# Raising the scheduling priority of attention steps by 300 places in a two-layer hybrid mixer

## The chip, the cores and the metric

The kernel runs on one core of a Trainium2 chip. The metric is device time in microseconds (us). A core has TensorE (PE, with its weight loads as PEld), VectorE (DVE), ScalarE (ACT), GpSimd (POOL) and SyncE (SP, here the issuer of most transfers). Each engine works through its own list of instructions in the order in which the compiler's scheduler wrote it down, and waits at the head of that list for semaphores.

## The reference

Two layers of a mixer on 512 tokens of x (plus 256 tokens of context), width 1024. Each layer projects the normalised input with `w_in`, runs three mixers side by side, gates them, and multiplies with `w_out`:

```python
oa = _rms(_diff_attend(qa, ka, va, lam), da_subln_g) * (1.0 - lam_init)
ob = _rms(_gqa_attend(qg, kg, vg).reshape(B, L, GQ_WIDTH), gq_out_g)
oc = _rms(_hyena(uh, filt, hy_short_w, hy_short_b, hy_bias), hy_out_g)
y = jnp.concatenate([oa * jax.nn.silu(ga), ob * jax.nn.silu(gg), oc * jax.nn.silu(gh)], axis=-1)
return y @ w_out
```

`_diff_attend` (DA below) has 4 heads whose attention matrix is softmax minus lambda times a second softmax; `_gqa_attend` (GQA) has 8 query heads over 2 key heads; `_hyena` is a gated long convolution, done here by matrix products. In layer 0 the context is a query too, in layer 1 only x is. Keys are the context and x together, 768 of them for a query of x.

## The kernel before

The work is float32, done as three matmuls on a high and a low half of each operand (lines L138, L139, L140 of `mm3`); `split` and `evac_split` make the halves, ACT the high one and DVE or POOL the low one (L152, L156, L581, L582). A layer's function projects one weight block after another (`proj_tok` into tiles named `pst`, `proj_feat` into `psf`), and after the last block multiplies the mixed heads with `w_out` into tiles named `px`.

Attention is written as generators. `gq_att` and `da_att` do one head and one block of 256 queries per step: scores `S` (six matmuls for each half block in DA, L628 and L629; nine in GQA), a maximum on DVE (L634), the exponential into `P` on ACT (L637), then `pv`. For each of three pairs of key blocks, `pv` transposes `P` with four matmuls into `T` (L648), splits `T` on ACT into `ph` (L581) and on DVE into `pl` (L582), and adds four matmuls from `ph` (L655, L656) and two from `pl` (L658) to `O`. In DA, `O` is squared on ACT (L972), read once more by DVE (L974), and a matmul `ms` (L977) sums squares over the partitions; `ms` uses the buffer of `O`. The pools `pT` and `pO` have one buffer each (L91, L92): a second `T` waits until both splits of the first are done, a new `O` until `ms` has been read.

Who comes first is settled in two stages. The code is traced in a fixed order: `att.tock()` at the head of each projection lets one or more attention steps be traced between projections, by a pace that `att.spread` sets; `slow.tick()` inside an attention step traces a piece of the modulation for the next layer; `bg` and `pre` hold hyena and next-layer work; `att.drain()` empties what is left before the `w_out` part. The scheduler then lists the instructions of each engine: of those that it holds ready it takes the one with the highest priority, and priority is the place in the traced order, the earlier the higher. So a projection traced after an attention step still comes ahead of it where the step's inputs are not there yet.

The `w_out` part reads the heads back from DRAM: `yT` tiles for blocks 0 to 7 by POOL's transfers straight to their place (L1089, L1094), blocks 8 to 14 by SP's transfers into `yld` (L1100), split by ACT (L1082) and DVE or POOL.

```python
            for i, kp in enumerate(klist):
                T = pT.tile([128, 2, 256], F32, tag="T", name="T")
...
                evac_split(ph, pl, T)
```

Of the kernel before, what the change touches and what calls it, by code (L numbers as in the profile page):

```python
# [3 lines left out]

# [30 lines left out]
class Background:  # L35


    def __init__(self):
        self.queue = deque()
        self.pace = self.due = 1.0  # L40

    def add(self, gen):
        self.queue.append(gen)
# [11 lines left out]
    def tick(self):  # L55
        while self.queue:
            try:
                next(self.queue[0])
                return
            except StopIteration:  # L60
                self.queue.popleft()
# [7 lines left out]
def hybrid_mixer(ctx: ExitStack, tc: tile.TileContext, a, out):  # L69
# [50 lines left out]

    bg = Background()
    slow = Background()
    att = Background()
    pre = Background()

    def col(l, c, n=1):
# [1372 lines left out]
```

## Time and profile before

| what | value |
|---|---|
| median of three runs | 1597.02 us (1595.21 to 1600.0) |
| the profiled execution, its own time | 1593.43 us |
| its span | 1591.7 us |
| mean granted clock of TensorE | 0.989 |
| PE busy | 1510.1 us, 95% |

The profiled execution is 3.6 us under the median, so a sum made against it stands 3.6 us lower than the time of a run. PE is the engine that is nearly always busy: 81.6 us of the span are left in which no matmul runs, and a gain or a loss by another order of the same work is a change of these 81.6 us.

### The profile page before, as it was taken

How to read it: one execution, taken by the hardware profiler on the slowest of the kernel's cores; microseconds unless marked ns; L12 is line 12 of the kernel's file. 1: busy time of each engine (PE TensorE's matmuls, PEld its weight loads, DVE VectorE, ACT ScalarE, POOL GpSimd, SP SyncE). 2: the span in 40 equal slices, each digit the busy share in tenths (PEclk: the TensorE clock that was granted, in tenths of full speed). 3: DMA queues.
4: the chain of work that ended last, by engine and by line, in shares of the span. 5: the costliest groups of instructions: out<-in, count | busy, mean ns of one | idle time of the engine just before them, and what ended most of it. 6: DMA issues, size and time to landing. Idle time of an engine off the chain costs nothing.

```text
span 1591.7 us, 29098 instructions
## 1 busy us (share of the span) xinstructions
PE 1510.1 (95%) x11126; PEld 1398.6 (88%) x11126; DVE 1127.6 (71%) x2222; ACT 830.9 (52%) x1673; POOL 415.6 (26%) x451
## 2 busy tenths in 40 slices
PE   5989999999999999998999999999999999898997
PEld 3768889999898989798999977888999998898997
DVE  6789667877776475777755378869877756768755
ACT  5645243555556555566653256334546556656643
POOL 0243443212212141113002114334222222214032
PEclk9999999999999999999999999999999999999999
DMA  9437676423435253315352334674422232115441
GB/s 344 145 111 263 192 222 200 129 76 96 143 102 169 93 159 117 113 48 195 117 179 94 93 108 145 213 229 146 152 75 87 87 97 87 57 51 182 130 133 70
DMA packets 105952, 216.87 MB, mean 136 GB/s; under 512 B 11345, under 2 KB 54291, under 8 KB 105812
## 3 DMA queue, kind: packets, MB, share of 16 engines
q1 hardware_dynamic: 95300, 178.56, 34.9%
q0 software_dynamic: 9936, 35.39, 7.3%
q8 instruction: 88, 1.44, 0.4%
q10 hardware_dynamic: 576, 1.05, 0.2%
q14 instruction: 52, 0.43, 0.1%
HBM read 174.45 MB, written 40.52 MB: 135 GB/s over the span
## 4 chain that ended last, share of the span: by engine, by line
PE 79%; DVE 9%; DMA 4%; issue 3%; ACT 3%; POOL 1%; SPq 0%; POOLq 0%; DVEq 0%; ACTq 0%
PE psf L138 7%; PE psf L139 7%; PE psf L140 7%; PE pst L138 6%; PE pst L140 6%; PE pst L139 6%; PE px L138 4%; PE px L140 4%; PE px L139 4%; PE T L648 4%; PE O L658 2%; PE O L655 2%; PE O L656 2%; PE S L138 2%; PE S L140 2%
## 5 line engine op out<-in xcount | busy, mean ns | idle before, releaser
L138 PE MATMUL psf<-hT,wh 128*128 128x512 f32 (+1 forms) x768 | 267.9, 353 | 8.8 <-DVE cv L687 5.0
L138 PE MATMUL pst<-wh,hT 128*128 128x256 f32 x960 | 273.8, 285 | 0.2
L139 PE MATMUL pst<-wl,hT 128*128 128x256 f32 x960 | 273.7, 285 | 0.0
L140 PE MATMUL pst<-wh,hT 128*128 128x256 f32 x960 | 273.6, 285 | 0.0
L139 PE MATMUL psf<-hT,wh 128*128 128x512 f32 (+1 forms) x768 | 268.4, 350 | 0.0
L140 PE MATMUL psf<-hT,wl 128*128 128x512 f32 (+1 forms) x768 | 268.2, 349 | 0.0
L156 DVE TENSOR_TENSOR wl<-raw,wh 128x1024 fp32r<-128x1024 f32 x136 | 174.6, 1285 | 40.1 <-ACT wh L152 38.7
L152 ACT ACTIVATE wh<-raw 128x1024 fp32r<-128x1024 f32 x136 | 143.5, 1056 | 90.1 <-PE psf L139 34.7
L140 PEld LDWEIGHTS pst<-wh,hT 128*128 128x128 f32 x960 | 183.9, 192 | 1.7 <-issue 1.7
L138 PEld LDWEIGHTS pst<-wh,hT 128*128 128x128 f32 x960 | 184.0, 192 | 1.6 <-issue 1.1
L139 PEld LDWEIGHTS pst<-wl,hT 128*128 128x128 f32 x960 | 183.9, 192 | 0.2
L138 PE MATMUL px<-wh,yT 128*128 128x256 f32 x640 | 181.6, 284 | 1.1 <-DMA yT<-yx 0.6
L140 PE MATMUL px<-wh,yT 128*128 128x256 f32 x640 | 181.6, 284 | 0.2 <-DVE yT L1083 0.2
L139 PE MATMUL px<-wl,yT 128*128 128x256 f32 x640 | 181.5, 284 | 0.0
L637 ACT ACTIVATE P<-S,sa 128x768 f32<-128x768 f32 (+1 forms) x160 | 130.2, 814 | 87.3 <-DVE sa L634 59.1
L138 PEld LDWEIGHTS psf<-hT,wh 128*128 128x128 f32 x768 | 146.3, 191 | 29.0 <-ACT kH L1029 3.2
L140 PEld LDWEIGHTS psf<-hT,wl 128*128 128x128 f32 x768 | 146.5, 191 | 17.9 <-issue 0.8
L139 PEld LDWEIGHTS psf<-hT,wh 128*128 128x128 f32 x768 | 146.9, 191 | 17.3 <-issue 1.2
L634 DVE TENSOR_REDUCE sa<-S 128x1 f32<-128x768 f32 (+1 forms) x160 | 134.6, 841 | 21.8 <-PE S L140 11.9
L582 DVE TENSOR_TENSOR pl<-T,ph 128x512 fp32r<-128x512 f32 x156 | 107.1, 687 | 49.0 <-ACT ph L581 44.2
L581 ACT ACTIVATE ph<-T 128x512 fp32r<-128x512 f32 x156 | 92.7, 594 | 86.5 <-PE T L648 85.6
L138 PEld LDWEIGHTS px<-wh,yT 128*128 128x128 f32 x640 | 122.1, 191 | 2.1 <-ACT pm L1152 0.9
(300 smaller groups left out, 3559.8 us busy)
## 6 DMA issues: line engine op xcount, KB each, us to landing
raw<-in_w_in SPq DMA_DIRECT2D x104, 512.0 KB, 4.1
adaw<-in_ada_w SPq DMA_DIRECT2D x32, 512.0 KB, 4.4
raw<-in_w_out SPq DMA_DIRECT2D x32, 512.0 KB, 3.8
tab<-in_inv POOLq DMA_DIRECT2D x20, 512.0 KB, 4.6
tab<-in_fwd POOLq DMA_DIRECT2D x18, 512.0 KB, 5.1
adaw<-in_ada SPq DMA_DIRECT2D x16, 512.0 KB, 10.7
yT<-yx POOLq DMA_DIRECT2D x16, 512.0 KB, 7.1
gl<-gd SPq DMA_DIRECT2D x60, 128.0 KB, 2.3
```

The lines of the kernel that those rows point to most:

```text
L138: i0 = PE.matmul(ps, sh, mh, start=first, stop=False)
L139: PE.matmul(ps, sh, ml, start=False, stop=False)
L140: return i0, PE.matmul(ps, sl, mh, start=False, stop=last)
L152: ACT.activation(hi, src, AF.Copy)
L156: last_lo[0] = e.tensor_tensor(out=lo, in0=src, in1=hi.bitcast(F32), op=ALU.subtract)
L581: ACT.activation(dh, ps, AF.Copy)
L582: return DVE.tensor_tensor(out=dl, in0=ps, in1=dh.bitcast(F32), op=ALU.subtract)
L634: DVE.tensor_reduce(out=nm, in_=S[:, :n], axis=AX.X, op=ALU.max, negate=True)
L637: ACT.activation(P[:, :n], S[:, :n], AF.Exp, bias=nm, accum_out=s)
L648: PE.transpose(T[:, kk, q * 128:(q + 1) * 128], aa[q][:, (2 * i + kk) * 128:(2 * i + kk + 1) * 128], ident)
L655: PE.matmul(O, vh, ph[:, kk], start=(i == 0 and kk == 0), stop=False)
L656: PE.matmul(O, vl, ph[:, kk], start=False, stop=False)
```

## The change

`Background` gets a tile context and a lift. Each step that the attention queue traces runs under a priority raised by 300 places, so everything that it traces (scores, softmax, transposes, the O matmuls, its loads and stores, and what `slow.tick()` adds in it) is ranked as if it stood 300 instructions earlier in the traced order. The three other queues keep a lift of 0. No instruction is added or taken away; line numbers behind L59 grow by two.

```diff
-    def __init__(self):
+    def __init__(self, tc=None, lift=0):
         self.queue = deque()
         self.pace = self.due = 1.0
+        self.tc, self.lift = tc, lift
...
             try:
-                next(self.queue[0])
+                with self.tc.high_priority(offset=self.lift) if self.lift else nullcontext():
+                    next(self.queue[0])
                 return
...
-    att = Background()
+    att = Background(tc, 300)
```

The lists of the engines differ from layer 0's first attention step on; between the two layers' attention they are nearly alike. Two places show how.

PE near the end of layer 1, the last two query blocks of DA, before: after the last transpose into `T_18296` come 26 matmuls of the w_out part (`px`), and then the O matmuls that read its high half `ph_18301`.

```order
L648 MATMUL T_18296<-ident_243,P_18242 128x128
L139 MATMUL px_18704<-wl_18693,yT_18455 128x256
L140 MATMUL px_18704<-wh_18692,yT_18455 128x256
L138 MATMUL px_18704<-wh_18692,yT_18457 128x256
...
L139 MATMUL px_18704<-wl_18687,yT_18447 128x256
L140 MATMUL px_18704<-wh_18686,yT_18447 128x256
L655 MATMUL O_18265<-ph_18301,vh_17443 128x256
L656 MATMUL O_18265<-ph_18301,vl_17444 128x256
L655 MATMUL O_18265<-ph_18301,vh_17443 128x256
L656 MATMUL O_18265<-ph_18301,vl_17444 128x256
```

On PE at the same place of the changed kernel, `px_18704` and `px_18807` have been done already, and the transposes, the O matmuls and the next transposes follow each other:

```order
L650 MATMUL T_18296<-ident_243,P_18210 128x128
L650 MATMUL T_18296<-ident_243,P_18242 128x128
L657 MATMUL O_18265<-ph_18301,vh_17443 128x256
L658 MATMUL O_18265<-ph_18301,vl_17444 128x256
L657 MATMUL O_18265<-ph_18301,vh_17443 128x256
L658 MATMUL O_18265<-ph_18301,vl_17444 128x256
L650 MATMUL T_18389<-ident_243,P_18333 128x128
L650 MATMUL T_18389<-ident_243,P_18365 128x128
L650 MATMUL T_18389<-ident_243,P_18333 128x128
L650 MATMUL T_18389<-ident_243,P_18365 128x128
L660 MATMUL O_18265<-pl_18302,vh_17443 128x256 x2
L650 MATMUL T_18404<-ident_243,P_18333 128x128
```

What moved: the px matmuls went ahead of the attention's last blocks, and nothing is left between a transpose and the matmuls that need its two splits. In the changed order no px stands between any of `T_18296`, `T_18389`, `T_18404`, `T_18419` and the O matmuls that follow; in that of before 15 or more stand behind each of the four.

ACT in layer 0, at the turn from projections to the w_out part, before: the split of the first loaded tile, `yT_10077<-yld_10075`, stands behind the exponential of `P_9402`, in front of the split `ph_9268` of an attention's transposes.

```order
L1029 ACTIVATE kH_9382<-kH_9382 64x256
L972 ACTIVATE sq_9111<-O_9095 128x256
L637 ACTIVATE P_9402,sa_9403<-S_9393,sa_9400 128x768
L1082 ACTIVATE yT_10077<-yld_10075 128x512
L581 ACTIVATE ph_9268<-T_9263 128x512
L978 ACTIVATE sq_9111<-ms_9115,epst_246 128x256
L637 ACTIVATE P_9416,sa_9417<-S_9407,sa_9414 128x768
L979 ACTIVATE sq_9111<-sq_9111 128x256
L1082 ACTIVATE yT_10082<-yld_10080 128x512
```

On ACT at the same place of the changed kernel both splits of loaded tiles stand in front of exponentials:

```order
L967 ACTIVATE P_9221<-P_9221,sa_9226 128x768
L1084 ACTIVATE yT_10077<-yld_10075 128x512
L639 ACTIVATE P_9239,sa_9240<-S_9230,sa_9237 128x768
L980 ACTIVATE sq_9111<-ms_9115,epst_246 128x256
L981 ACTIVATE sq_9111<-sq_9111 128x256
L1084 ACTIVATE yT_10082<-yld_10080 128x512
L639 ACTIVATE P_9253,sa_9254<-S_9244,sa_9251 128x768
L967 ACTIVATE P_9253<-P_9253,sa_9258 128x768
L639 ACTIVATE P_9402,sa_9403<-S_9393,sa_9400 128x768
L1014 ACTIVATE qT_9573<-pst_9513 128x512
L639 ACTIVATE P_9416,sa_9417<-S_9407,sa_9414 128x768
L583 ACTIVATE ph_9268<-T_9263 128x512
```

What moved: `yT_10077` stands ahead of the exponentials of `P_9239`, and `yT_10082` ahead of that of `P_9253`, both of an earlier attention step than before. On SP, `yld_10075` was issued directly after the load `gl_9045`; in the changed list it stands behind a weight load and the store `yx0_9<-y_8891`, which waits for POOL.

Elsewhere on PE: after `T_14039` (GQA, layer 1) stood 25 rows of matmuls before its O matmuls, now none; after `T_14407` 19, now none; after `T_15587` 23, now none; `T_14182` follows the transposes before it with two rows between. Between the last projection matmul of `pst_9318` and its own transposes (DA, layer 0) stood 45 rows of matmuls, now 13.

## Rows read from the trace of the kernel before

**Rows 1.** the page: busy time, share and instructions of each engine.

```profile
PE 1510.1 (95%) x11126; PEld 1398.6 (88%) x11126; DVE 1127.6 (71%) x2222; ACT 830.9 (52%) x1673; POOL 415.6 (26%) x451
```

**Rows 2.** windows: busy us of PE, PEld, DVE, ACT, POOL; granted clock; DMA.

```profile
300.00:400.00 100.00, 100.00 (x775) 94.75 (x773) 74.52 (x173) 56.61 (x126) 20.61 (x20) 1.00 0.34 105
...
700.00:800.00 100.00, 91.68 (x716) 88.19 (x715) 78.63 (x162) 69.84 (x147) 21.25 (x38) 0.97 0.41 133
...
1300.00:1400.00 100.00, 93.34 (x709) 88.63 (x709) 66.89 (x128) 57.55 (x109) 27.44 (x38) 0.98 0.25 79
...
1500.00:1530.00 30.00, 30.00 (x253) 29.93 (x252) 15.20 (x26) 13.12 (x25) 0.73 (x1) 1.00 0.66 203
740.00:765.00 25.00, 20.36 (x141) 18.95 (x139) 20.35 (x43) 17.58 (x35) 9.38 (x17) 0.86 0.79 264
```

**Rows 3.** what PE waited for: us in total, times, longest.

```profile
PE O L655 <- ACT ph L581: 6.2, 6, 3.0
...
PE O L658 <- DVE pl L582: 3.3, 7, 1.2
...
PE T L648 <- DVE pl L582: 1.5, 3, 0.9
```

**Rows 4.** timeline of PE: start, us, line, tiles; idle before it and releaser.

```profile
1370.82 0.60 PE L648 MATMUL T<-ident,P 128*128 128x128 f32 x4
1372.10 0.38 PE L655 MATMUL O<-ph,vv 128*128 128x256 f32 x1 [0.69 <-ACT ph L581]
...
1373.14 0.80 PE L658 MATMUL O<-pl,vv 128*128 128x256 f32 x2 [0.20 <-DVE pl L582]
```

**Rows 5.** timeline of ACT, same stretch.

```profile
1371.45 0.60 ACT L581 ACTIVATE ph<-T 128x512 fp32r<-128x512 f32 x1 [0.90 <-PE T L648]
```

**Rows 6.** timeline of DVE, same stretch.

```profile
1372.39 0.69 DVE L582 TENSOR_TENSOR pl<-T,ph 128x512 fp32r<-128x512 f32 x1
```

**Rows 7.** timeline of PE, layer 0, third attention head of DA.

```profile
746.78 0.60 PE L977 MATMUL ms<-sq,ones 128*128 128x256 f32 x2
748.00 0.39 PE L655 MATMUL O<-ph,vh 128*128 128x256 f32 x1 [0.63 <-ACT sq L978]
...
749.26 0.60 PE L648 MATMUL T<-ident,P 128*128 128x128 f32 x4
...
753.53 0.39 PE L655 MATMUL O<-ph,vh 128*128 128x256 f32 x1 [2.96 <-ACT ph L581]
```

**Rows 8.** timeline of ACT, same stretch.

```profile
751.05 0.63 ACT L1082 ACTIVATE yT<-yld 128x512 fp32r<-128x512 f32 x1 [1.92 <-DMA yld<-yx]
...
752.89 0.59 ACT L581 ACTIVATE ph<-T 128x512 fp32r<-128x512 f32 x1
```

**Rows 9.** timeline of SP: the first two loads of yld.

```profile
726.13 0.44 SPq L1100 DMA_DIRECT2D yld<-yx  x1
...
742.05 0.75 SPq L1100 DMA_DIRECT2D yld<-yx  x1
```

**Rows 10.** timeline of POOL: first and last issue of eight loads of yT.

```profile
736.94 1.14 POOL L1089 DMA_DIRECT2D yT<-yx  x2 [2.57 <-PE pst L140]
...
742.10 1.07 POOL L1089 DMA_DIRECT2D yT<-yx  x2
```

**Rows 11.** timeline of PE, layer 0: last projection matmul and its transposes.

```profile
703.94 0.28 PE L140 MATMUL pst<-wh,hT 128*128 128x256 f32 x1
...
708.24 0.66 PE L1050 MATMUL pst<-ident,t 128*128 128x128 f32 x4 [1.49 <-POOL t L1046]
```

**Rows 12.** timeline of PE, layer 1: two waits outside the round trips.

```profile
1326.30 0.47 PE L138 MATMUL psf<-hT,wh 128*128 128x512 f32 x1 [1.04 <-DVE kL L1027]
...
1333.90 0.39 PE L138 MATMUL S<-kk,qh 128*128 128x256 f32 x1 [0.74 <-ACT P L637]
```

**Rows 13.** timeline of PE, layer 1: the turn at ms.

```profile
1435.52 0.40 PE L658 MATMUL O<-pl,vh 128*128 128x256 f32 x2
...
1438.10 0.70 PE L977 MATMUL ms<-sq,ones 128*128 128x256 f32 x2 [1.31 <-DVE y L974]
```

More of the change, by code (lines that the diff above doesn't have):

```diff
@@ L2 @@
 from collections import deque
-from contextlib import ExitStack
+from contextlib import ExitStack, nullcontext
 import numpy as np
```

## The prediction

> **What bounds the kernel now.** The page's busy times come first: PE is busy for 1510.1 of 1591.7 us, 95%, DVE 71%, ACT 52% [rows 1]. The windows come next, to see where the other 81.6 us lie. Between 300 and 400 us PE has no gap at all, and in the tail at 1500 to 1530 none either; between 700 and 800 it is busy for 91.68 us and between 1300 and 1400 for 93.34 [rows 2]. So the projections alone keep PE full, and the gaps lie where the two layers' attention runs. The waits of PE name them: `O` for `ph` 6.2 us, `O` for `pl` 3.3, the next `T` for `pl` 1.5 [rows 3]. Together 11.0 us: the round trip from PE to ACT and DVE and back that each set of transposes makes. A change of order moves only gaps, so the question is which round trips have other matmuls beside them.
>
> **What a bare round trip costs.** At 1370.82 four transposes start; ACT's split starts at 1371.45 and takes 0.60, DVE's starts at 1372.39 and takes 0.69; the first O matmul starts at 1372.10 and the one from `pl` at 1373.14 [rows 4 to 6]. So `ph` is usable 1.28 us after the first transpose, `pl` 2.32 us after it, and the buffer of `T` is free again at the same moment, 2.31 us. Of this PE's own work is 0.44 (four transposes at 0.11 apart) and 0.48 (four O matmuls at 0.12): with nothing between, PE idles 0.84 us before the first O matmul and 0.56 before the `pl` pair, 1.40 in all.
>
> **The change, term by term.** No instruction is added or removed, so busy time is left as it is, and the sum is made of gaps.
>
> Round trips. I went down PE's list of each kernel, adding 0.11, 0.12 or 0.23 us for a matmul of 128, 256 or 512 columns, and held each O matmul and each next `T` to the 1.28, 2.32 and 2.31 us. Before, 23 matmuls are held up, by 9.5 us in all; the trace has 11.0 at the same waits [rows 3], so the walk is near the chip's result, a little low. After, 34 are held up, by 19.2. Where: 5.0 us in the last two query blocks of layer 1, where the lists show no px between transposes and O, and where the window was gapless [rows 2]; 4.9 in the GQA of layer 1 (1.4 each at `T_14039` and `T_15587`, 1.3 at `T_14182`, 0.8 at `T_14407`); 3.4 instead of 1.0 at the first DA head of layer 0; 2.6 less elsewhere. That is +9.7, and scaled by 11.0/9.5 it is **+11.2**. Its lower end is +9.7; its upper end takes the widest measured excess over a bare trip, 3.0 us (below), once more: +14.
>
> The Trainium skill, Perfetto Trace Analysis, section Matmuls, says that independent groups of matmuls should rotate through PSUM banks, so that the evacuation of one overlaps the next group's matmuls. The trace agrees: with one buffer for `T` there is no second transpose to start, and what hides the evacuation is other groups alone. By that rule a list that groups attention's matmuls together loses, which is the sign of the sum above.
>
> Turns at `ms`. From `ms` at 746.78 to the next O matmul at 748.00 is 1.22 us [rows 7], of which PE works 0.24: about 1.0 of idling where nothing stands between. The list of before has two such turns with under 0.5 us of work between, that of after three: **+1.2** with the shorter cover of one more.
>
> Transposes of the DA projections. Their input goes through DVE and POOL: from the last projection matmul at 703.94 to the transposes at 708.24 are 4.3 us [rows 11]. For `pst_9318` the list of after has 1.64 us of matmuls there where before had 5.6: 4.3 less 0.12 and 1.7 leaves **+2.4** (0 if the input is ready sooner than in that row, as DVE was busy with other work in it).
>
> ACT at the loaded tiles. Before, ACT stood still for 1.92 us at L1082, waiting for the load of `yld`; behind it stood a split of `T`, which began at 752.89, so that PE got its O matmul at 753.53, 4.27 us after the transposes at 749.26 [rows 7, 8]. A bare trip is 1.28: the excess is 3.0. The load was late because SP issued `yld` at 742.05 (an earlier one at 726.13) behind eight loads of 512 KB that POOL had issued from 736.94 to 742.10 [rows 9, 10], with the DMA engines at 0.79 of their time [rows 2]. After, two such splits stand ahead of exponentials of an earlier step, and the first load too is issued behind the store that waits for POOL, so into the same burst. One held load cost 3.0; I take two at 3.0 each in place of one, **+3.0**. Ends: 0 if the second load lands while ACT is held by the first, +6 if the exponentials, which stand farther from PE's matmuls than a split does, hold the scores' two buffers as well.
>
> Gains. Two waits outside the round trips, 1.04 and 0.74, stand where the list of after has scores and projections earlier: **-1.8** [rows 12]. The wait of 1.31 at `ms` [rows 13] is behind more matmuls: **-1.3**. No other cover grows where the trace had a wait.
>
> Sum: 11.2 + 1.2 + 2.4 + 3.0 - 1.8 - 1.3 = **+14.7**. Against the profiled execution that is 1593.4 + 14.7 = 1608; against the median, 3.6 us above it, **1612**. I leave the clock out of the sum: where PE idled 18% of a stretch, at 740 to 765, its granted clock was 0.86 [rows 2], so one more such stretch of 25 us costs 25 x 0.14 = 3.5 us; that goes to the range.
>
> **The rivals.**
> Faster. The lift brings attention's splits and exponentials ahead of weight splits in ACT's and DVE's lists, so that the chip's trips come to their bare length, and each trip starts sooner. For it: DVE is busy 71% and the excess at 753.53 is queueing. If all the waits for `ph` and `pl` vanished, 11.0 us would be gained: 1586. Against it: of those 11.0 the bare trips explain 9.5, so queueing is only some 1.5 of them, and a shorter queue gives no cover. It decides if the short covers of the list (34 against 23) are filled on the chip, that is if O's waits for `ph` and `pl` in the new trace are under 8 us. The Trainium skill, Perfetto Trace Analysis, section Optimization Strategy, advises to make the dependencies behind a gap start sooner; that is this rival's mechanism, and the row at 753.53 agrees with it in one place.
>
> No change. PE's gaps move: what the tail loses, an earlier place gets back, because each lifted step gives up its place to a projection of the same length. For it: the 81.6 us of gaps have many causes, and I have priced only some. Against it: it needs 10 more of gains, and I find 3.1 in the rows. Time: 1597, within 4.8 us.
>
> Much slower. ACT's two held loads take 6 instead of 3 more, PE idles over a longer stretch, and two stretches of 25 us run at 0.86: 14.7 + 3 + 7 = +25, 1622. It decides if ACT's wait for `yld` is over 4 us in total around 750.
>
> **How the numbers follow.** A measurement here can tell about 0.3%, 4.8 us, from no change. Chances: forecast (1605 to 1618) 0.53, much slower 0.20, no change 0.14, faster 0.13. Slower by over 0.3%: 0.73; within: 0.14; faster: 0.13. The range 1592 to 1628 leaves out most of the faster case below and the far end of the much slower one above; the forecast's own range is 1605 to 1618.
>
> **What would show it.** Right: O's waits for `ph` and `pl` and T's for `pl` rise from 11.0 to about 20 in the waits of PE; gaps of about 1.4 us between transposes and O in the last 20 us of attention in layer 1, where px filled them; the px part after the last O unchanged in length; a wait of ACT for `yld` in layer 0 in front of an exponential. Wrong: waits under 8 us there; PE busy over 95% between 1500 and 1530; or a new wait of 5 us or more at a place not named, most likely scores waiting for `P` or a projection waiting for a split.

## The result and the profile after

The changed kernel takes 1625.09 us (median of four runs, 1622.44 to 1627.03), the kernel before 1597.58: a ratio of 1.0171 with a 95% interval of 1.0148 to 1.0194, or 27.5 us more. The sign was forecast, and the time lies in the range of 1592 to 1628. The size was not: 14.7 us were in the sum, and the forecast's own range ended at 1618. The profiled executions differ by 33.6 us of span (1625.3 against 1591.7), since that of after was the slowest of its four runs and that of before the fastest of its own.

The page's busy times, as in [rows 1]:

```profile
PE 1527.0 (94%) x11126; PEld 1407.6 (87%) x11126; DVE 1123.4 (69%) x2222; ACT 833.0 (51%) x1673; POOL 419.0 (26%) x451
```

PE is busy for 17 us longer with the same matmuls, and the rest of the span, in which no matmul runs, went from 81.6 to 98.3 us. Not only the gaps grew, then: matmuls themselves took longer, in part because the mean granted clock fell from 0.989 to 0.983. The windows (columns as in [rows 2]), the last two between the two layers' attention:

```profile
300.00:400.00 100.00, 99.98 (x774) 94.72 (x772) 74.46 (x171) 57.01 (x127) 21.15 (x20) 1.00 0.32 103
...
700.00:800.00 100.00, 91.99 (x724) 88.94 (x723) 72.83 (x153) 63.46 (x132) 22.11 (x38) 0.97 0.39 130
1300.00:1400.00 100.00, 94.48 (x689) 88.17 (x688) 63.68 (x110) 57.04 (x102) 26.45 (x34) 1.00 0.29 92
1530.00:1560.00 30.00, 26.60 (x199) 24.73 (x198) 13.96 (x23) 13.75 (x26) 0.74 (x1) 0.94 0.60 197
1050.00:1070.00 20.00, 15.14 (x61) 12.42 (x60) 11.35 (x17) 6.93 (x10) 5.34 (x4) 0.83 0.64 212
1090.00:1110.00 20.00, 17.04 (x122) 16.87 (x121) 15.45 (x32) 6.85 (x14) 7.16 (x7) 0.83 0.49 147
```

Between 300 and 400 nothing changed, and 700 to 800 and 1300 to 1400 are no worse than in [rows 2]; the windows of 100 us cut at other places of the work, since everything slid. The tail is what the reader should compare: 30.00 of 30 before, 26.60 of 30 here at 1530 to 1560, at a clock of 0.94. Between 1050 and 1110 the clock is 0.83 in two stretches of 20 us.

What PE waited for, where [rows 3] had 6.2, 3.3 and 1.5 for `O` and `T`:

```profile
PE S L630 <- ACT P L639: 9.7, 11, 2.5
...
PE O L657 <- ACT ph L583: 7.9, 10, 1.2
...
PE yps L140 <- ACT Z L763: 4.9, 1, 4.9
PE T L650 <- DVE pl L584: 4.8, 6, 1.3
...
PE O L660 <- DVE pl L584: 2.4, 5, 0.9
...
PE pst L1052 <- POOL t L1048: 1.9, 1, 1.9
...
PE pst L140 <- DVE vl L584: 1.9, 2, 1.6
...
PE px L140 <- ACT P L639: 1.7, 1, 1.7
```

The round trips rose from 11.0 to 7.9 + 2.4 + 4.8 = 15.1 us. The largest wait is one that [rows 3] did not show: scores waiting for their buffer, which the exponential `P` must read first, 9.7 us (in the kernel before 2.9 in DA, and 1.4 in GQA, which is gone). All PE waits but those for a DMA went together from 52.6 to 71.6 us.

To see where, I took the time from each matmul's start to the next one's, less 0.109, 0.120 or 0.227 us for up to 128, 256 or 512 columns, and summed what is left over five parts of the program. It holds gaps and slow clock alike. The first row is the sum in us, the others the difference to it:

```
                      start  layer 0   between   layer 1   tail   sum
before                 24.5     15.8      19.9      20.7    0.6   81.4
after                  +1.1    +12.6      +6.0      +7.8   +6.3  +33.9
lift_layer0            -0.8    +12.3      +6.7      +2.8   -0.3  +20.7
lift_layer1            +1.7     -1.9      +0.9      +9.3   +7.5  +17.6
lift_no_drain          +0.5    +13.1      +0.5      +7.3   -0.0  +21.3
no_drain_layer1        +4.1    +12.6      +6.4      +6.5   -0.0  +29.5
store_on_pool          +2.3    +11.8      -2.6      +7.1   +5.8  +24.4
scores_unlifted        +1.1    +18.5      +2.0     +12.7   +2.3  +36.7
pv_unlifted            -1.0    +20.6      -0.0     +28.9  +11.9  +60.5
lift_30                +1.3     -4.8      +1.8      +7.0   -0.3   +4.9
lift_100               -1.3     +9.3      +3.2      +7.7   -0.0  +18.8
lift_1000              +1.4    +20.0      -0.3     +19.6  +14.6  +55.3
ysplit_pool_after      -0.4    +12.9      +1.4      +9.4   +7.4  +30.7
ysplit_pool_before     +2.1     -2.8      +2.2      +0.4   -0.1   +1.8
```

"Layer 0" is its attention and w_out part, "between" the hyena and projection work up to layer 1's first transposes, "tail" begins with the transposes of the last two query blocks. The differences fit those of the spans (33.9 and 33.6 us for the changed kernel). The expectations below speak of 9.6 and 6.5 us between the layers and of 6.5 in the tail; by this table it is 6.0 and 6.3. These are single executions: in the first part nothing is changed, and it varies by -1 to +4.

### The profile page after: what moved, and what is told of

Its sections match the earlier page's. It is cut to its first block, busy times and chain, and to the rows that moved or that the text cites. A ratio compares the mean times of both kernels' runs of the same rounds, so it can differ in the third digit from the quotient of the medians.

```text
span 1625.3 us, 29141 instructions
## 1 busy us (share of the span) xinstructions
PE 1527.0 (94%) x11126; PEld 1407.6 (87%) x11126; DVE 1123.4 (69%) x2222; ACT 833.0 (51%) x1673; POOL 419.0 (26%) x451
## 4 chain that ended last, share of the span: by engine, by line
PE 79%; DVE 8%; DMA 4%; ACT 3%; issue 3%; POOL 1%; SPq 0%; ACTq 0%; DVEq 0%; POOLq 0%
PE psf L140 7%; PE psf L141 7%; PE psf L142 7%; PE pst L140 7%; PE pst L141 7%; PE pst L142 7%; PE px L140 5%; PE px L142 5%; PE px L141 4%; PE T L650 3%; PE O L657 2%; PE O L660 2%; PE O L658 2%; PE S L140 1%; PE S L141 1%
## 5 line engine op out<-in xcount | busy, mean ns | idle before, releaser
L636 DVE TENSOR_REDUCE sa<-S 128x1 f32<-128x768 f32 (+1 forms) x160 | 134.6, 841 | 23.5 <-PE S L142 17.3
```

Source lines behind the costliest of these rows:

```text
L636: DVE.tensor_reduce(out=nm, in_=S[:, :n], axis=AX.X, op=ALU.max, negate=True)
```

## The experiments

Their line numbers lie up to four above those of the kernel before. Where an interval is given it is the 95% interval of the ratio to the kernel before, which was timed again beside each group of runs (medians of 1594.28 to 1597.58 us).

**The lift in one layer.**

```diff
         full = l == 0
+        att.lift = 300 if l == 0 else 0
```

> The lift of 300 in layer 0 only, 0 in layer 1. Theory A (lost cover: matmuls that stood inside the round trips of transposes are gone): going down PE's list by the same spacings gives 10.7 us of held-up matmuls against 9.5 before, so +1.4, with +2.4 at the transposes of the DA projections and +3 at the loaded tiles: about +7, 1604 to 1605. Theory B (PE meets a lifted instruction in its list whose inputs or buffer are not there, scores above all, and later unlifted work is reshuffled with it): the changed kernel lost 12 us at the places of layer 0's attention and 9.6 us more between the two layers' attention, where nothing is lifted; both would stay, +20, about 1618.

> The lift of 300 in layer 1 only, so that every list up to layer 1's attention is that of the kernel before. Theory A: 19.4 us of held-up matmuls against 9.5, +11.5, with +1.2 at the turn of ms: about +13, 1610. Theory B: the changed kernel lost some 11 us from layer 1's first attention step to the end, and nothing of the 9.6 us between the layers should be lost here: about +10, 1608. If the 9.6 us between the layers were not caused by layer 0's lift they would be seen here too, about 1618.

Layer 0 alone: 1616.49 us, 1.0138 (1.0118 to 1.0158). Layer 1 alone: 1609.74, 1.0087 (1.0070 to 1.0104). The first is Theory B's number, the second lies between both theories and is near A's. PE's waits in layer 0 alone:

```profile
PE S L631 <- ACT P L640: 11.2, 12, 2.6
...
PE yps L140 <- ACT Z L764: 4.9, 1, 4.9
...
PE O L658 <- ACT ph L584: 3.7, 6, 1.2
```

and in layer 1 alone:

```profile
PE O L658 <- ACT ph L584: 10.7, 13, 2.1
...
PE O L661 <- DVE pl L585: 5.1, 9, 1.8
...
PE S L631 <- ACT P L640: 3.3, 6, 0.9
```

The two losses have different causes. In layer 1 the lift costs round trips (10.7 + 5.1 and 1.8 for `T`, 17.6 in all, where the walk down the list gave 19.4), and scores wait no more than before. In layer 0 round trips fall to 8.0 in all (2.96 of the 11.0 before were the wait behind the held load, [rows 7]), and it is scores that wait. The 4.9 us at `Z`, in work that nothing lifts, come with layer 0's lift.

**The tail.** No lift for the steps that `att.drain()` traces; in the second kernel the line reads `300 - 300 * l`, so that only layer 1's drain goes without.

```diff
+        att.lift = 0
         att.drain()
```

> The lift of 300 everywhere except for the attention steps that are traced when the queue is emptied behind the last projection. Theory A: the px matmuls are back between transposes and O at the end of layer 1, 14.9 us of held-up matmuls instead of 19.2 and none in the last heads: 5 to 7 us less than the changed kernel, 1618 to 1620. Rival: the loss at the tail comes from elsewhere (late inputs), and the time stays at 1625.

> The lift of 300 everywhere except for the steps traced when the queue is emptied in layer 1. If the losses are local and add up, only the 6.5 us in the last two query blocks of layer 1 come back, and the 6.5 us between the two layers' attention stay: about 1618 to 1619. If the run without the lift in both drains won its 11 to 14 us in layer 1 alone: 1612 to 1614.

Without the lift in both drains: 1611.78, 1.0103 (1.0081 to 1.0124). In layer 1's drain only: 1622.29, 1.0162 (1.0135 to 1.0188). In both, the tail's 6.3 us are gone (-0.0 in the table): that loss is the lifted steps of layer 1's last heads. But the whole run gained only 2.8 us from it in the median, less than these intervals can tell, and the larger gain of the first kernel came from elsewhere: the table puts 5.5 us of it into the part between the layers, where nothing is lifted. My expectation of 1618 to 1620 for it was right in its mechanism and missed this.

**What the lift is put on.** Scores at the old priority, everything else lifted; then, in a second kernel, transposes, splits and O matmuls at the old priority, scores and softmax lifted. The first part of the diff is of the one, the second of the other:

```diff
+            with tc.high_priority(offset=-300):
+                S = pS.tile([128, 1024], F32, tag="S", name="S")
...
+                with tc.high_priority(offset=-300):
+                    O = pv(aa, kl_, ...
```

> The lift of 300 for softmax, transposes and O, but the scores' matmuls at their old priority. Theory B (PE comes to scores in its list before their buffer is free): the waits of scores for P fall from 9.7 us to about 3, 1616 to 1619. Theory A (lost cover alone): 17.6 us of held-up matmuls against 19.2, so 1623 to 1625.

> The lift of 300 for scores and softmax, but transposes, their splits and the O matmuls at their old priority. Theory A: the list has 39.1 us of held-up matmuls against 19.2, which at the share that the chip showed for the changed kernel (15.1 of 19.2) is +16: about 1641. Theory B: what is lifted, the scores, still waits, and the round trips are no worse on the chip than with the lift: 1620 to 1628.

Scores unlifted: 1624.88, 1.0168 (1.0142 to 1.0193), no gain. Their wait did not fall to 3 us but rose:

```profile
PE S L632 <- ACT P L641: 12.3, 14, 3.2
```

So Theory B as I put it, that PE meets the scores too early because they are lifted, falls: the buffer is late, not the scores early. Transposes unlifted: 1650.53, 1.0339 (1.0319 to 1.0359), 10 us beyond Theory A's 1641 and far from B's 1620 to 1628.

```profile
PE S L630 <- ACT P L639: 14.5, 16, 1.6
PE O L657 <- ACT ph L583: 13.1, 13, 4.4
PE T L650 <- DVE pl L584: 8.0, 12, 1.2
PE ms L981 <- DVE y L978: 6.5, 5, 1.6
```

Scores and softmax then run ahead, and the transposes come in bunches later; the walk had 39.1 us of held-up matmuls, the chip shows 13.1 + 2.9 + 8.0 = 24.0, with 6.5 at `ms` and, those of GQA counted in, 19.1 at scores besides. Lost cover in PE's list is a real price, and the walk ranks kernels roughly: 9.5, 19.2 and 39.1 by the list stand against 11.0, 15.1 and 24.0 in the trace, and elsewhere 10.7 against 8.0 (layer 0 alone), 19.4 against 17.6 (layer 1 alone), 24.5 against 17.3 (lift of 1000). From run to run the list is level with the trace or up to two thirds above it. Only in the kernel before is the list clearly lower, because its 11.0 hold the wait behind the held load.

**The size of the lift.** One number is changed, here for 100:

```diff
-    att = Background(tc, 300)
+    att = Background(tc, 100)
```

> The lift at 30. Lost cover by the list: 11.6 us of held-up matmuls against 9.5 before and 19.2 at 300; by what the runs so far gave of such a difference (0.45) +1: 1598. If any new order costs what the changed kernel lost outside the round trips (scores, the hyena part between the layers), whatever the size of the lift: 1608 to 1615.

> The lift at 100. Lost cover: 12.4 us of held-up matmuls, +1 to +2: 1599. If the loss grows evenly with the lift, a third of that at 300: 1606. If any new order costs as much as at 300 outside the round trips: 1610 to 1618.

> The lift at 1000 instead of 300. Theory A: 24.5 us of held-up matmuls against 19.2 with the lift of 300, +6: about 1631. Theory B: the waits of scores for their buffer grow with the lift (2.9 us before, 9.7 with 300, 15 or more here): about 1635 to 1645.

With 30: 1596.78, 1.0009 (0.9995 to 1.0024), no difference. With 100: 1615.17, 1.0126 (1.0106 to 1.0146). With 1000: 1648.79, 1.0336 (1.0311 to 1.0361). PE's waits with 30, and then with 100:

```profile
PE O L657 <- ACT ph L583: 5.7, 8, 1.2
...
PE S L630 <- ACT P L639: 4.5, 6, 1.3
```

```profile
PE S L630 <- ACT P L639: 9.1, 9, 2.9
...
PE yps L140 <- ACT Z L763: 5.0, 1, 5.0
```

The walk has 11.6 us for 30 and 12.4 for 100, hardly different, and their times lie 18 us apart. At 100 it is again scores (9.1) and `Z` (5.0) that carry the loss, not round trips (12.6). So not every new order costs, since that of 30 is another order too and free in the median (in its profiled execution layer 0 is 4.8 us shorter and layer 1 7.0 longer, so parts balance); and the loss does not grow evenly with the lift. With 1000 the tail alone loses 14.6 us, and the time is above both expectations; DA's scores waited for 11.9 us and not 15, the round trips took 17.3.

**The held loads.** The two first loaded tiles of layer 0 split by POOL instead of ACT, in each kernel:

```diff
+            if l == 0 and i in (12, 13):
+                POOL.tensor_copy(h, src)
+            else:
                 ACT.activation(h, src, AF.Copy)
```

> The changed kernel, with the high halves of layer 0's first two loaded tiles (yT from yld) made by POOL instead of ACT. If ACT's wait of 2.8 us for the load is what holds the exponentials, the waits of scores for P of 2.5 and 1.2 us near 757 go and the scores' waits fall from 9.7 to about 6: 1620 to 1622 unless POOL, which now waits in ACT's place, holds the next head's keys. If the scores wait for ACT's own work, 9.7 and 1625 stay.

> The kernel before with the same two splits on POOL. The wait of O for ph of 3.0 us at 753 was blamed on ACT's wait for the load; if so it is gone, 2 to 4 us, 1593 to 1595, and this is a version faster than both. If the split was only one of several things ACT had to do there: 1597.

Here is what the changed kernel does at this place: SP, ACT and PE on the timeline.

```profile
748.04 0.32 SPq L984 DMA_DIRECT2D yx<-y  x1
748.45 0.91 SPq L1102 DMA_DIRECT2D yld<-yx  x2
```

```profile
755.33 0.63 ACT L1084 ACTIVATE yT<-yld 128x512 fp32r<-128x512 f32 x1 [2.81 <-DMA yT<-yg]
```

```profile
756.89 0.38 PE L630 MATMUL S<-kH,qT 128*128 128x256 f32 x1 [2.46 <-ACT P L639]
...
759.10 0.58 PE L630 MATMUL S<-kH,qT 128*128 128x256 f32 x1 [1.24 <-ACT P L639]
```

SP issues the two `yld` loads directly behind the store, in the middle of POOL's loads (issued from 746.63 to 750.60). ACT waits 2.81 us at the split, by the profile until a load of that burst (`yT<-yg`) had landed, with the exponentials behind it, and PE stands at scores for 2.46 and 1.24 us. That the burst holds ACT is shown; how much of it the store added is not. With POOL in ACT's place the changed kernel takes 1620.59, 1.0162 (1.0141 to 1.0183), and the long waits are gone, but the sum of scores' waits is hardly smaller:

```profile
PE S L630 <- ACT P L639: 9.2, 11, 1.3
```

The longest is 1.3 instead of 2.5 us. So ACT's held split made these two waits, 3.7 us, and their removal bared others: round trips rose from 15.1 to 19.1 us. The time is that of the expectation, 1620 to 1622, but by luck: layer 0 loses 12.9 us in the table where the changed kernel loses 12.6, and the gain lies between the layers (1.4 instead of 6.0), where the new lists have a wait for `Z` of 2.1 instead of 4.9. The kernel before with the same edit: 1595.46, 1.0012 (0.9993 to 1.0030), no faster:

```profile
PE yps L138 <- ACT Z L761: 5.3, 1, 5.3
...
PE O L655 <- ACT ph L581: 3.8, 6, 1.6
```

The wait of `O` for `ph` fell from 6.2 to 3.8 (the one of 3.0 us is gone), and in that execution the wait of `yps` for `Z` is 5.3 us, where the kernel before has 2.0. This kernel has no lift at all. In the table layer 0 gains 2.8 us, as the expectation had it, and the start and the part between the layers lose 2.1 and 2.2.

**The wait at Z.** In the changed kernel PE, POOL and SP read as follows, with POOL of the kernel before as the third listing:

```profile
1063.14 0.58 PE L140 MATMUL yps<-tab,Z 128*128 128x256 f32 x1 [4.86 <-ACT Z L763]
```

```profile
1044.45 1.68 POOL L709 TENSOR_TENSOR ux<-cv 128x512 f32<-128x512 f32 x1 [3.28 <-DVE cv L689]
...
1054.76 2.54 POOL L754 TENSOR_TENSOR m<-UW,H 128x512 f32<-128x512 f32 x2 [5.03 <-DMA H<-sp1x]
```

```profile
1030.43 1.61 POOL L707 TENSOR_TENSOR ux<-cv 128x512 f32<-128x512 f32 x1 [1.35 <-DVE cv L687]
...
1039.01 2.55 POOL L752 TENSOR_TENSOR m<-UW,H 128x512 f32<-128x512 f32 x2 [1.38 <-DMA H<-sp1x]
```

```profile
1046.16 0.33 SPq L710 DMA_DIRECT2D hyu<-ux  x1
1046.59 0.55 SPq L749 DMA_DIRECT2D H<-sp1x  x1
```

POOL waits 3.28 us before it multiplies `ux`, and 1.35 in the kernel before, because the two steps of DVE's convolution stand one and three places later in DVE's list; SP, which holds the store of `ux` at the head of its queue, issues the load of `H` behind it; POOL's product with `H` starts 8.2 us after that issue (1046.59 to 1054.76) and after a wait of 5.03 us (1.38 before), and PE waits 4.86. The granted clock of this stretch was 0.83. The runs divide by this order: the five kernels in which POOL waits 3.28 us for the convolution and SP issues the store (the changed one, lift_layer0, no_drain_layer1, lift_100 and, without any lift, ysplit_pool_before) have waits for `Z` of 4.2 to 5.3 us; the eight with a shorter wait there have 0.3 to 2.1. The experiment lets POOL issue layer 1's stores of `ux` itself:

```diff
-                SP.dma_start(hyd[4 * l + b][isx]["u"], u)
+                (POOL if l else SP).dma_start(hyd[4 * l + b][isx]["u"], u)
```

> The changed kernel, with layer 1's store of the hyena product ux issued by POOL, which computes it, instead of SP. If the wait for Z between the layers is this chain (DVE's convolution later in its list, so ux on POOL later, so SP held at the store, so the load of H behind it lands late), the wait of yps for Z falls from 4.9 us to 2 or less, POOL's wait for H of 5.0 to 1.4 or less, and the stretch runs at a higher clock: 1618 to 1622. If the load of H is late for another reason, 4.9 and 1625 stay.

It took 1621.33, 1.0151 (1.0131 to 1.0171). PE's wait, and the same stretch's window:

```profile
PE yps L140 <- ACT Z L763: 1.4, 1, 1.4
```

```profile
1050.00:1070.00 20.00, 18.60 (x99) 15.78 (x98) 14.62 (x21) 9.38 (x14) 9.17 (x7) 1.00 0.74 238
```

The wait fell from 4.9 to 1.4, although POOL still waits 3.28 us for the convolution; it no longer waits for `H`, and the clock stays at 1.00. The chain is shown at its place; of the whole run's time 3.8 us are gone, within the expected 1618 to 1622, though the two intervals overlap.

No version was faster than the kernel before.

## Why the prediction was right in sign and half the size

**The premise on busy time.** That "busy time is left as it is, and the sum is made of gaps" failed. By the two pages, 16.9 of the 33.6 us between the profiled executions are busy time of the same matmuls, and 16.7 are gaps. That the gaps come near the 14.7 of the sum is luck, as the terms show.

**Round trips, +11.2.** Right in mechanism for layer 1, too large: +4.1 was measured (11.0 to 15.1). By place, these waits rose in layer 1 from 5.4 to 10.0 us before the tail and from nothing to 2.6 in the tail, and fell in layer 0 from 5.6 to 2.5. The tail's size is nearly as forecast: 5.0 for the round trips and a part of the 1.2 at `ms` were in the sum, +6.3 was measured, and taking the lift from that drain took it back. But the waits are only 3.4 of it (2.6, then 0.6 behind `ms` and 0.2 at px); the rest is matmuls that took longer, which the sum did not price. Here is PE at the place of the second pair of order listings:

```profile
1551.12 0.66 PE L650 MATMUL T<-ident,P 128*128 128x128 f32 x4 [1.18 <-DVE pl L584]
...
1552.83 0.39 PE L657 MATMUL O<-ph,vh 128*128 128x256 f32 x1 [0.62 <-ACT sq L980]
...
1553.95 0.41 PE L657 MATMUL O<-ph,vh 128*128 128x256 f32 x1
1554.16 0.41 PE L658 MATMUL O<-ph,vl 128*128 128x256 f32 x1
...
1556.97 0.39 PE L657 MATMUL O<-ph,vh 128*128 128x256 f32 x1 [0.69 <-ACT ph L583]
1557.19 0.28 PE L658 MATMUL O<-ph,vl 128*128 128x256 f32 x1
1557.31 0.28 PE L657 MATMUL O<-ph,vh 128*128 128x256 f32 x1
...
1558.43 0.38 PE L140 MATMUL px<-wh,yT 128*128 128x256 f32 x1 [0.23 <-ACT pm L1154]
```

Waits of 1.18, 0.62 and 0.69 us stand where px stood before. Behind the first two, O matmuls are 0.21 us apart (1553.95 to 1554.16), and behind 1557.19 again 0.12: 256 columns in 0.21 us is the lower of TensorE's two levels, 1.2 GHz, and 0.12 the higher, 2.4. The step that failed here is the scaling of the walk by 11.0/9.5. The 11.0 hold the wait of 2.96 that the prediction itself put down to the held load, and priced a second time in that term. The kernel before with POOL in ACT's place has 3.8 + 4.2 + 1.5 = 9.5 us at these waits, the walk's own number; against that the changed kernel's 15.1 are +5.6 of the walk's +9.7. Why the rest was not seen stays open; that it was absorbed where PE had waited for something else already was argued, not shown.

**Turns at `ms`, +1.2.** As forecast: the waits of `O` for `sq` rose from 0.6 to 1.8.

**Scores.** The sum had no term for the scores' own round trip (six or nine matmuls, a maximum on DVE, an exponential on ACT, two buffers), only the held loads. At DA's scores the wait rose by 6.8 us, from 2.9 to 9.7 (that of GQA's, 1.4, went), and in the runs by layer it comes with layer 0's lift. Of this 3.7 us are the held loads, in place of the 2.96 at `O` before: two of them cost 0.7 more, for which +3.0 was forecast, and without them layer 0 was no faster. The other 3.1 us, shorter waits, are not settled: that scores wait only because they are lifted is excluded, and that lifted splits and softmax pieces crowd ACT and DVE there was argued only. Four of these waits (3.3 us) lie between 640 and 670, and there ACT and DVE are no busier (20.4 and 22.2 us of 30) than in the same window before (20.4 and 25.3). So the largest part of the loss, layer 0's 12.6 us, stays in part unexplained.

**Between the layers, nothing costed.** I wrote that the lists there are nearly alike and gave it no price. Two convolution steps that stand a little later on DVE were enough for most of +6.0 us: 2.9 more of a wait for `Z`, the rest at a lower clock and in shifted waits. In the runs by layer it comes with layer 0's lift and is absent with layer 1's; but lift_no_drain, scores_unlifted, pv_unlifted and lift_1000, which lift in layer 0 as well, lose -0.3 to 2.0 there. It is undone by another queue for the store, and turns up as a wait of 5.3 us without any lift. So it goes with the place of those two steps in the list, which a reordering elsewhere can move.

**Transposes of the DA projections, +2.4.** The wait appeared (1.9 us at L1052), but the 1.5 us that the kernel before has at another tile went: +0.4.

**Gains.** Of the -1.8, the 1.4 of GQA's scores went (0.74 of it was priced), but projections wait for `kL` as long as before, 2.2 us. The 1.3 at `ms` went in layer 1 as forecast, while in layer 0 the wait at `ms` rose from 0.4 to 2.8. New ones that I had not priced came from projections and px held behind attention's work: `pst` for `vl` 1.9, px for `P` 1.7.

**Clock.** Left out of the sum, and it is a part of the longer matmuls. By the mean granted clocks, 0.989 and 0.983, the two profiled executions lost 17.5 and 27.6 us of full clock: 10 us more, at most, of the 16.9. The same two stretches in the kernel before:

```profile
1034.00:1054.00 20.00, 18.01 (x76) 14.56 (x75) 15.43 (x23) 9.52 (x14) 7.09 (x6) 0.91 0.78 234
1074.00:1094.00 20.00, 16.93 (x129) 16.55 (x129) 16.67 (x39) 7.46 (x15) 7.21 (x7) 0.91 0.49 145
```

After, 1050 to 1070 and 1090 to 1110 stand at 0.83, and the tail at 0.94 instead of 1.00. Each time PE had waited before it fell; but in the second stretch it had waited 3.0 us in both kernels, so the wait alone does not tell 0.83 from 0.91. Nor is the clock the main cause of the whole loss: another execution of the changed kernel had a mean of 0.989, as the profiled one of before, and a span of 1620.7 us, 29.0 more. The time is near that of the much-slower rival, 1622, by luck and without its cause: its mark, ACT's wait for `yld` over 4 us around 750, was not reached (2.81).

**The other rivals.** Faster: its mark was under 8 us of round trips; 15.1 were seen. No change: the gaps that moved did not balance here, as every part of the table is longer (with the lift of 30 they do).

## What to carry to other kernels

When only an order changes, go down the list of the engine that bounds and price every kind of round trip that crosses it, not only the one that the trace shows waiting now; a cover that no wait betrays is still a cover. Such a walk ranks orders roughly, but its differences came out up to about twofold too large here, and a wait with another cause must be taken out of the measured sum before the walk is scaled by it. Places where one late instruction holds an in-order queue with a load behind it (a store at SP's head, a split at ACT's) are worth finding, since a reordering far away can trip them.

## What the runs showed that I had not expected

A lift of 30 places is free and one of 100 costs some 20 us (1596.78 and 1615.17, both against 1594.28), so the price is not even in the size. Work that was not lifted lost 6 us. And the two layers' losses, +21.1 and +14.4 us in separate runs (1616.49 and 1609.74 less 1595.39), are together 8 us more than the 27.5 of the whole change, where the three intervals leave some 6 us of doubt: an order's costs need not add up.
